# One encoder layer on one core: the first two feed-forward tiles in an order of their own, gate and up alternating

## The chip, the cores and the metric

One core of a Trainium2 chip runs the whole program. The time is that of one execution on the device in microseconds, from the first to the last instruction with what lies around them. The kernel before was run three times: 1383.03, 1385.15 and 1387.94 us, median 1385.15.

## The reference, cut to what matters

One layer is applied to 1088 tokens (1024 of a new stream, 64 of a running one), model width 1024, feed-forward width 2816, all in 32-bit floats:

```
xn   = rmsnorm(x, norm_mix)
proj = xn @ w_in                       # split into three kinds of token mixers
mix  = concat(hgrn2(...), s5(...), rglru(...))
x    = x + mix @ w_out                 # out projection
xn2  = rmsnorm(x, norm_ffn)
hid  = silu(xn2 @ w_gate) * (xn2 @ w_up)
x    = x + hid @ w_down
y    = rmsnorm(x, norm_final)
```

The change touches the first products of the input projection (the S5 branch's input u), the end of the out projection with the RMS factors of the second norm, and the first two of the 22 feed-forward tiles of 128 columns.

## The kernel before, in words

The tokens stand in the free dimension, in three groups: 0 and 1 of 384 tokens, 2 of 320. The model width is eight slices of 128 partitions. A 32-bit value is split into a rounded high part (written by a copy on ACT) and the low rest (a subtraction on DVE). A product of weights and activations is then three rounds of matmuls into one PSUM tile, called j = 0, 1, 2: high by high, high weight by low activation, low weight by high activation (`dense`, L128; `product`, L1363). TensorE's instructions run in the order in which they are written; a dependency from each to the one before fixes it (L67). The other engines' orders are made by the scheduler from the order in the text, an instruction's priority, and when it can run; `first()`, `soon()` and `tc.high_priority(offset)` move what stands inside them ahead by so many instructions (400 for WPRIO). A tile belongs to a tag with a number of buffers, and an instruction that writes a new tile waits until one of them is free.

**Start.** Group 2 is first. Its x comes in four transfers of two slices each; `xsplit` (L324) splits each slice into xh (ACT) and xl (DVE). `weights_part` (L110) fetches half a weight tile (four slices, 256 KB) into a buffer with tag raw (three of them), ACT makes the high part whi and a negated copy in wlo, and a DMA of POOL's queue adds the weights onto it. The loop at L1147 sets the order of loads and splits: the halves of the first u tile stand behind slices 1 and 5, both halves of the second at the end. `uproj` (L350) makes one product after the other, 24 matmuls each; for group 2 the rounds run over the first four slices and then the last four.

**Out projection and second norm.** `outproj` (L174) makes eight output slices; those of slices 0 and 1 are done together, then each slice's product, an addition on DVE, its square on ACT and its sum on DVE (`square_sum`, L205). For a group, `row_sums` (L216) adds over the partitions on PE, `inv_rms` (L232) makes one over the root in a chain of some fifteen small DVE instructions, `spread` (L248) puts it across the partitions with two matmuls. The chain of group 0 lies in `finish` (L983), beside the out projection of group 1; that of group 1 beside the out projection of group 2 (loop at about L1334: row sums and chain at step 1, spread at step 3).

**Feed-forward, first pair of tiles.** Two tiles of weights and groups 0 and 1 are multiplied as a 2 by 2 block matrix with seven products in place of eight (`quad`, L1390), on operands that are halves of the scaled activations, or their sums and differences: b11, b22, d1 = b21 - b11, s = b11 + b22, d2 = b12 - b22, r2 = b21 + b22, r1 = b11 + b12. `operand` (L1299) makes each in four slices: an addition into a buffer with tag xT (four of them, also used for t, u, the squares and x2prep), the high part on ACT, the low part on DVE. b11, d1, b22 and s are made beside the out projection of group 2 (`preps`, L1317), d2, r2 and r1 behind it (`preps_late`, L1325); the additions of r2 and r1 run on POOL, all others on DVE. `scaled` (L1292) multiplies the rows by the RMS factors first. In `quad` the four parts of a weight block are loaded once (`raws`, L1370: two in raw, two in rw), their five sums and differences are made on DVE (L1396), and `wsplit` (L1356) splits them; whi and wlo have five buffers. The order of products is b11, b22, s, d1, d2, r2, r1. t, the copy of the first sum, is made on ACT (L1407) and then changed by the second and third product; d1 is added onto the first sum's PSUM tile, so it comes behind the copy. For the first pair the quad of gate comes first, then the chain, spread and `x2prep` (L258) of group 2, then the quad of up, then four `plain` products (L1382) of group 2 with newly fetched weights. For all later pairs the group-2 products lie inside the quad.

Of the kernel before, what the change touches and what calls it, by code (L numbers as in the profile page):

```python
# [58 lines left out]
def trunk(ctx: ExitStack, tc: tile.TileContext, I: dict, O: list):  # L59
# [114 lines left out]
    def outproj(gi, pool, xpool, xbufs, psd):  # L174
# [8 lines left out]
        sacc = pool.tile([128, TMAX], F32, tag="sil" if gi == 2 else "sacc", name="sacc", bufs=2)  # L183
# [94 lines left out]
    with ExitStack() as ph1:  # L278
# [71 lines left out]
        def uproj(gi, parts):  # L350
            T = GROUPS[gi]["T"]
            hi, lo = xn[gi]
            for m in range(2):
                o = ps_mm()
                dense(o[:, :T], parts[m], lambda k: (hi[:, k, :T], lo[:, k, :T]),
                      key=(lambda s: (s[1] == 2, s[0] // 4, s[1])) if gi == 2 else None)
                with tc.high_priority(offset=WPRIO):
                    for s0, n, dst in u_cols(gi, m):
                        A.copy(dst, o[:, s0:s0 + n].rearrange("p (c t) -> p t c", t=8))
# [623 lines left out]
        def finish():  # L983
# [10 lines left out]
            diags = inv_rms(0, sc)  # L994
# [152 lines left out]
        for k in range(NK):  # L1147
# [3 lines left out]
            if k in (1, 5):  # L1151
                part(0, k - k % 4)
        part(1, 0)
        part(1, 4)
# [162 lines left out]
    def preps():  # L1317
# [5 lines left out]
        yield from operand("s", halves(bigtile("o_s")), b11, b22, OP.add)  # L1323

    def preps_late():  # L1325
        yield from operand("d2", halves(bigtile("o_d2")), b12, b22, OP.subtract)
# [6 lines left out]
    for i, _ in enumerate(outproj(2, p2, p2, 4, ps_d)):  # L1333
        if i == 1:  # L1334
            with first():
                diags = inv_rms(1, row_sums(1, [sums[1]], ps_t))
        if i == 3:
            spread(1, diags, ps_t, sums[1])
# [51 lines left out]
    def quad(src, m, post, with_g2):  # L1390
# [30 lines left out]
        if with_g2:  # L1421
            plain(w11 + single(a12), post, m)
            plain(single(a21) + w22, post, m + 1)
# [11 lines left out]
    for fi, nf in enumerate(ffg):  # L1435
# [18 lines left out]
        for m in range(f0, f0 + nf, 2):  # L1454
            sil = [p2.tile([128, NTOK], F32, tag="sil", name="sil", bufs=2) for _ in range(2)]
            quad(I["w_gate"], m, gated, m > 0)
            if m == 0:
                with first():
                    diags = inv_rms(2, row_sums(2, [sums[2]], ps_t))
                spread(2, diags, ps_t, sums[2])  # L1460
                weave(x2prep(2, p2, (bigtile("x2h2"), bigtile("x2l2"))))
            quad(I["w_up"], m, upped, m > 0)
            if m == 0:
                for src, post in ((I["w_gate"], gated), (I["w_up"], upped)):
                    for i in range(2):
                        plain(weights(src[i], False), post, i)
# [116 lines left out]
```

## Time and profile before, and how to read it

| | |
|---|---|
| median of three runs | 1385.15 us |
| the profiled execution | 1381.88 us |
| its span, first to last instruction | 1380.1 us |
| mean granted clock of TensorE | 0.95 of full speed |
| PE, DVE, ACT, POOL busy | 92%, 66%, 48%, 16% |

A line of a timeline has the start in us, the length in us, the engine, the line of the kernel, the operation, the tile written and those read, the shape and the number of instructions merged; in brackets is the idle time before it and what ended it. A line of groups has the count, the busy time in us and the mean of one in ns, then idle time. Matmuls overlap their neighbours, so the distance of starts, and not their length, is what one costs. PEclk is the granted clock as a share of 2.4 GHz.

### The profile page before, as it was taken

The page shows a single profiled execution, that of the slowest core. Times are in us where ns is not written, and L with a number is a line of the kernel's source. Part 1 is how long each engine was busy: PE and PEld are TensorE (multiplying, and loading weights), DVE is VectorE, ACT ScalarE, POOL GpSimd, SP SyncE. Part 2 cuts the span into 40 slices and gives each one's busy share as a digit, 9 for nine tenths or more (in the row PEclk, how much of TensorE's full clock was granted, in tenths as well). Part 3 has the DMA queues.
Part 4 walks back from the last instruction along what each step waited for, and adds up shares of the span by engine and source line. Part 5 has one row for each costly group of instructions (what it writes and reads, how often), then busy time and mean ns, then how long its engine had stood idle before and what let it go on. Part 6 is the DMA issues. An engine that isn't in the chain of part 4 may idle for free.

```text
span 1380.1 us, 21112 instructions
## 1 busy us (share of the span) xinstructions
PE 1275.0 (92%) x7608; PEld 1214.8 (88%) x7608; DVE 913.5 (66%) x2206; ACT 660.0 (48%) x1288; POOL 224.2 (16%) x278
## 2 busy tenths in 40 slices
PE   7987998989988999759999999999999999999995
PEld 7876897878777889659999999999999999999985
DVE  9875798857766668976475437543763476346687
ACT  7766657768885444434243224412442243133463
POOL 2334354424342000020100000010001000100000
PEclk8997999999998899779999999999999999999997
DMA  9977687768884346303812551254125412631543
GB/s 285 287 148 180 138 172 147 172 142 177 164 188 107 104 162 212 116 15 96 164 39 71 117 96 38 77 107 92 55 71 110 80 54 77 107 78 62 184 141 111
DMA packets 94330, 170.60 MB, mean 124 GB/s; under 512 B 11425, under 2 KB 31473, under 8 KB 94225
## 3 DMA queue, kind: packets, MB, share of 16 engines
q1 hardware_dynamic: 70080, 108.26, 25.9%
q0 software_dynamic: 24144, 60.99, 25.0%
q8 instruction: 60, 0.98, 0.3%
q14 instruction: 46, 0.37, 0.1%
HBM read 134.76 MB, written 33.86 MB: 122 GB/s over the span
## 4 chain that ended last, share of the span: by engine, by line
PE 51%; DVE 3%; DMA 1%; issue 1%; ACT 0%; DVEq 0%; ACTq 0%
PE q L76 51%; DMA res<-st 1%; DVE wlo L122 1%; DVE u L1429 0%; DVE dg L243 0%; DVE x1r L1353 0%; DVE hl L1452 0%; DVE u L1430 0%; DVE sil L1450 0%; ACT whi L1359 0%; DVE sacc L214 0%; DVE sc L150 0%; DVE sc L149 0%; DVE sc L148 0%; DVE x1r L1480 0%
## 5 line engine op out<-in xcount | busy, mean ns | idle before, releaser
L117 ACT CAST whi<-raw 128x512 fp32r<-128x512 f32 (+1 forms) x232 | 139.5, 607 | 101.0 <-PE q L76 40.9
L76 PE MATMUL mm<-xh,whi 128*128 128x384 f32 (+1 forms) x480 | 168.8, 360 | 17.9 <-ACT whi L117 9.9
L76 PE MATMUL q<-hl,whi 128*128 128x384 f32 (+1 forms) x528 | 173.2, 332 | 2.7 <-DVE hl L1452 2.7
L76 PE MATMUL q<-hh,whi 128*128 128x384 f32 (+1 forms) x528 | 172.9, 331 | 2.1 <-ACT hh L1451 1.7
L76 PE MATMUL mm<-xl,whi 128*128 128x384 f32 (+1 forms) x480 | 159.6, 340 | 4.5 <-DVE xl L332 4.5
L120 POOL DMA_DIRECT2D wlo<-in_w_in_dram x112 | 99.4, 971 | 211.9 <-ACT wlo L119 180.1
L1482 DVE COPY st<-q 128x384 f32<-128x384 f32 x80 | 41.4, 524 | 134.3 <-PE q L76 118.5
L1493 POOL DMA_DIRECT2D res<-st x40 | 34.0, 851 | 585.9 <-DVE st L1482 499.7
L76 PEld LDWEIGHTS mm<-xh,whi 128*128 128x128 f32 x480 | 95.3, 200 | 25.5 <-ACT whi L117 10.5
L76 PE MATMUL q<-hh,wlo 128*128 128x384 f32 (+1 forms) x528 | 111.7, 330 | 0.0
L1359 ACT CAST whi<-raw 128x512 fp32r<-128x512 f32 x128 | 78.1, 621 | 67.4 <-PE q L76 53.9
L1360 DVE TENSOR_TENSOR wlo<-raw,whi 128x512 fp32r<-128x512 f32 x128 | 87.5, 685 | 29.6 <-ACT whi L1359 14.2
L76 PEld LDWEIGHTS q<-hl,whi 128*128 128x128 f32 x528 | 100.3, 190 | 4.9 <-DVE hl L1452 4.9
L76 PE MATMUL q<-x2l,whi 128*128 128x320 f32 x352 | 103.8, 309 | 0.0
L76 PE MATMUL q<-x2h,whi 128*128 128x320 f32 x352 | 103.8, 309 | 0.0
L76 PEld LDWEIGHTS q<-hh,whi 128*128 128x128 f32 x528 | 100.1, 190 | 4.0 <-ACT hh L1451 3.6
L122 DVE TENSOR_TENSOR wlo<-raw,whi 128x512 fp32r<-128x512 f32 (+1 forms) x120 | 80.1, 672 | 34.3 <-ACT whi L117 29.4
L76 PEld LDWEIGHTS mm<-xl,whi 128*128 128x128 f32 x480 | 94.8, 198 | 9.0 <-DVE xl L332 6.0
L76 PE MATMUL mm<-xh,wlo 128*128 128x384 f32 (+1 forms) x480 | 93.4, 335 | 6.1 <-DMA wlo<-in_w_in_dram 6.0
L1396 DVE TENSOR_TENSOR sm<-raw 128x512 f32<-128x512 f32 x66 | 45.6, 691 | 75.0 <-DMA raw<-in_w_up_dram 57.3
L76 PEld LDWEIGHTS q<-hh,wlo 128*128 128x128 f32 x528 | 91.6, 190 | 0.0
L76 PEld LDWEIGHTS mm<-xh,wlo 128*128 128x128 f32 x480 | 82.5, 193 | 8.9 <-DMA wlo<-in_w_in_dram 8.7
(467 smaller groups left out, 2930.8 us busy)
## 6 DMA issues: line engine op xcount, KB each, us to landing
raw<-in_w_in_dram SPq DMA_DIRECT2D x112, 256.0 KB, 4.3
wlo<-in_w_in_dram POOLq DMA_DIRECT2D x112, 256.0 KB, 6.0
res<-st POOLq DMA_DIRECT2D x40, 544.0 KB, 6.0
raw<-in_w_down_dram SPq DMA_DIRECT2D x56, 256.0 KB, 2.7
raw<-in_w_out_dram SPq DMA_DIRECT2D x48, 256.0 KB, 3.1
raw<-in_w_gate_dram SPq DMA_DIRECT2D x48, 256.0 KB, 2.9
raw<-in_w_up_dram SPq DMA_DIRECT2D x48, 256.0 KB, 3.0
xg<-in_x_dram SPq DMA_DIRECT2D x8, 512.0 KB, 6.3
```

Of the source, the lines that this page charges most:

```text
L76: in_order(PE.matmul(out, lhsT, rhs, start=start, stop=stop, **kw).ins)
L117: ins = A.copy(hi[:, :n, :], raw[:, :n, :]).ins
L120: G.dma_start(lo[:, :n, :], src[:, h0:h0 + n, :], accum_op=OP.add)
L122: tt(lo[:, :n, :], raw[:, :n, :], hi[:, :n, :].bitcast(F32), op=OP.subtract)
L1359: A.copy(hi, src)
L1360: tt(lo, src, hi.bitcast(F32), op=OP.subtract)
L1396: tt(t_, a, b, op=op)
L1482: (A.copy if gi == 1 else V.tensor_copy)(st[:, t0:t0 + T], o[:, :T])
L1493: nc.gpsimd.dma_start(res[:, dm, :], st, accum_op=OP.add)
```

## The change

- The tile that holds the sum of squares of group 2 is taken from tag hh instead of sil.
- `uproj` for group 2 makes both products together: round 0 of the first four slices for both, of the last four for both, then round 1 for both, then round 2 for both. The load order alternates: first half of tile 0 behind slice 1, first half of tile 1 behind slice 3, second halves behind slices 5 and 7.
- The chain of group 0 in `finish` stands in `soon()`.
- The additions of s and d2 run on POOL.
- Row sums and chain of group 1 move to step 0 of the out projection of group 2, the spread to step 1, in `first()`.
- The first pair of tiles is made by a new function, `opening`, once for gate and once for up, in alternation, one product each per step. Its order is b11, d1, b22, s, d2, r2, r1. Each product fetches its own parts (alternately into rw and raw); the sums of weights are made on POOL. Row sums and chain of group 2 come before step 2, the spread before step 3, and x2prep behind all steps.

```diff
-        sacc = pool.tile([128, TMAX], F32, tag="sil" if gi == 2 else "sacc", name="sacc", bufs=2)
+        sacc = pool.tile([128, TMAX], F32, tag="hh" if gi == 2 else "sacc", name="sacc", bufs=4 if gi == 2 else 2)
...
+            os = [ps_mm() for _ in range(2)]
+            if gi == 2:
+                for ks, js in ((range(4), (0,)), (range(4, 8), (0,)), (range(8), (1,)), (range(8), (2,))):
+                    for m in range(2):
+                        for j in js:
+                            for k in ks:
+                                mm(os[m][:, :T], parts[m][k][j == 2], acts(k)[j == 1],
+                                   start=(j == 0 and k == 0), stop=(j == 2 and k == 7))
...
             sc = row_sums(0, [sums[0]], ps_mx)
-            diags = inv_rms(0, sc)
+            with soon():
+                diags = inv_rms(0, sc)
...
-            if k in (1, 5):
-                part(0, k - k % 4)
-        part(1, 0)
-        part(1, 4)
+            if k in (1, 3):
+                part(k // 2, 0)
+            if k in (5, 7):
+                part(k // 2 - 2, 4)
...
-        yield from operand("s", halves(bigtile("o_s")), b11, b22, OP.add)
+        yield from operand("s", halves(bigtile("o_s")), b11, b22, OP.add, G)
...
-        yield from operand("d2", halves(bigtile("o_d2")), b12, b22, OP.subtract)
+        yield from operand("d2", halves(bigtile("o_d2")), b12, b22, OP.subtract, G)
...
     for i, _ in enumerate(outproj(2, p2, p2, 4, ps_d)):
+        if i == 0:
+            with first():
+                diags = inv_rms(1, row_sums(1, [sums[1]], ps_t))
         if i == 1:
             with first():
-                diags = inv_rms(1, row_sums(1, [sums[1]], ps_t))
-        if i == 3:
-            spread(1, diags, ps_t, sums[1])
+                spread(1, diags, ps_t, sums[1])
...
+    def opening(src, post):
+        bufs = [0]
+        def fresh(dm, k):
+            bufs[0] += 1
+            pool, tag, n = ((wp, "raw", 3), (p2, "rw", 2))[bufs[0] % 2]
+            t_ = pool.tile([128, 4, 128], F32, tag=tag, name="raw", bufs=n)
+            nc.sync.dma_start(t_, src[dm][:, k:k + 4, :])
+            return t_
+        def summed(a, b, op):
+            with first():
+                x_, y_ = fresh(*a), fresh(*b)
+                G.tensor_tensor(x_, x_, y_, op=op)
+                return wsplit(x_)
+        a11, a12, a21, a22 = (0, 0), (0, 4), (1, 0), (1, 4)
+        oa, ob, oc = ps_q(), ps_q(), ps_q()
+        t_ = temp("t")
+        product(oa, summed(a21, a22, OP.add), "b11")
+        with first():
+            A.copy(t_, oa[:, :TMAX])
+        yield
+        product(oa, weights_part(src[1], 4)[0], "d1", False)
+        with first():
+            post(1, 0, oa[:, :TMAX])
+        yield
+        product(ob, summed(a11, a12, OP.add), "b22")
...
+        product(oc, summed(a11, a22, OP.add), "s")
...
+        product(ob, weights_part(src[0], 0)[0], "d2", False)
...
+        for x_, y_, name, acc, m, g in ((a12, a22, "r2", oa, 0, 0), (a21, a11, "r1", ob, 1, 1)):
+            o = ps_q()
+            product(o, summed(x_, y_, OP.subtract), name)
+            u = temp("u")
...
+            if m:
+                quad(I["w_gate"], m, gated)
+                quad(I["w_up"], m, upped)
+                continue
+            both = [opening(I["w_gate"], gated), opening(I["w_up"], upped)]
+            for i in range(7):
+                if i == 2:
+                    with first():
+                        diags = inv_rms(2, row_sums(2, [sums[2]], ps_t))
+                if i == 3:
+                    with first():
+                        spread(2, diags, ps_t, sums[2])
+                    run2 = x2prep(2, p2, (bigtile("x2h2"), bigtile("x2l2")))
+                for g in both:
+                    next(g)
+            for _ in run2:
+                pass
+            for src, post in ((I["w_gate"], gated), (I["w_up"], upped)):
+                for i in range(2):
+                    plain(weights(src[i], False), post, i)
```

## Rows read from the trace of the kernel before

**Rows 1.** The page, part 1: busy time, share of the span, instructions.
```profile
PE 1275.0 (92%) x7608; PEld 1214.8 (88%) x7608; DVE 913.5 (66%) x2206; ACT 660.0 (48%) x1288; POOL 224.2 (16%) x278
```

**Rows 2.** Busy time by stage: stretch, its length, each engine (instructions), PEclk, DMA share, GB/s.
```profile
0.00:24.60 24.60, 16.65 (x73) 14.47 (x74) 21.72 (x137) 14.90 (x30) 8.79 (x28) 0.72 0.91 265
...
500.00:535.70 35.70, 32.40 (x175) 31.00 (x173) 28.69 (x65) 16.86 (x35) 0.00 (x0) 0.95 0.58 189
...
566.70:600.30 33.60, 12.66 (x38) 9.06 (x36) 31.29 (x53) 15.14 (x31) 11.11 (x9) 0.61 0.15 52
600.30:634.40 34.10, 28.23 (x140) 27.46 (x141) 25.79 (x62) 13.54 (x26) 0.00 (x0) 0.88 0.19 55
634.40:681.00 46.60, 44.77 (x278) 43.84 (x276) 23.43 (x47) 15.10 (x33) 6.26 (x8) 1.00 0.66 128
```

**Rows 3.** PE's waits, 566 to 635 us: total us, times, longest us.
```profile
PE q L76 <- ACT t L1407: 14.2, 2, 12.1
PE q L76 <- issue: 5.0, 1, 5.0
PE q L76 <- DVE dg L243: 3.8, 1, 3.8
```

**Rows 4.** Timeline of ACT, 599 to 605 us.
```profile
599.38 0.51 ACT L1307 CAST o_r<-xs 128x384 fp32r<-128x384 f32 x1 [0.76 <-POOL xs L1305]
599.80 0.47 ACT L1407 COPY t<-q 128x384 f32<-128x384 f32 x1
```

**Rows 5.** Timeline of PE, 561 to 690 us.
```profile
568.15 0.86 PE L76 MATMUL q<-o_b,wlo 128*128 128x384 f32 x4
...
600.32 2.93 PE L76 MATMUL q<-o_d,whi 128*128 128x384 f32 x8 [12.14 <-ACT t L1407]
...
604.33 1.91 PE L76 MATMUL q<-o_d,whi 128*128 128x384 f32 x8
...
619.64 1.55 PE L76 MATMUL q<-o_b,whi 128*128 128x384 f32 x8
...
621.72 1.55 PE L76 MATMUL q<-o_s,whi 128*128 128x384 f32 x8
```

**Rows 6.** Timeline of PE, 0 to 55 us.
```profile
20.76 1.04 PE L76 MATMUL mm<-xh,whi 128*128 128x320 f32 x4
...
24.58 0.34 PE L76 MATMUL mm<-xh,whi 128*128 128x384 f32 x1
```

**Rows 7.** Timeline of PE, 500 to 690 us.
```profile
514.76 0.41 PE L76 MATMUL mx<-dg,ones_r 128*128 128x384 f32 x1 [1.39 <-DVE sc L241]
...
516.90 0.52 PE L76 MATMUL mm<-mh,whi 128*128 128x384 f32 x1
```

**Rows 8.** The same view, around row sums and spread of group 1.
```profile
542.84 0.72 PE L76 MATMUL q<-ones,sacc 128*128 128x1 f32 x6
...
551.72 0.44 PE L76 MATMUL q<-dg,ones_r 128*128 128x384 f32 x1 [1.01 <-DVE dg L243]
```

**Rows 9.** Groups of DVE instructions, 536 to 635 us, shapes kept apart.
```profile
L264 DVE SCALAR_TENSOR_TENSOR xT<-x,cols,sacc 128x320 f32<-128x320 f32 x8 | 4.1, 549 | 0.0
L1396 DVE TENSOR_TENSOR sm<-raw 128x512 f32<-128x512 f32 x6 | 4.1, 687 | 0.4 <-DMA raw<-in_w_up_dram 0.4
```

**Rows 10.** The tile o_r, 580 to 606 us: ns min/median/max, first and last start.
```profile
L1308 DVE TENSOR_TENSOR o_r<-xs,o_r x8: 545/1342/1346, 592.9 to 600.2; 128x384 fp32r<-128x384 f32 x8
```

**Rows 11.** Timeline of DVE, 540 to 690 us.
```profile
576.39 0.61 DVE L1295 SCALAR_TENSOR_TENSOR x<-x,cols,sacc 128x384 f32<-128x384 f32 x1
...
582.41 1.49 DVE L1308 TENSOR_TENSOR o_s<-xs,o_s 128x384 fp32r<-128x384 f32 x3
...
592.88 7.82 DVE L1308 TENSOR_TENSOR o_r<-xs,o_r 128x384 fp32r<-128x384 f32 x8
```

**Rows 12.** Timeline of POOL, 592 to 600 us.
```profile
593.04 6.31 POOL L1305 TENSOR_TENSOR xs<-x,x 128x384 f32<-128x384 f32 x5 [0.49 <-DVE o_d L1308]
```

**Rows 13.** DMA issues, 536 to 635 us: count, KB each, median us to landing.
```profile
raw<-in_w_gate_dram SPq DMA_DIRECT2D x10, 256.0 KB, 2.8
```

More of the change, by code (lines that the diff above doesn't have):

```diff
@@ L352, in uproj @@
             hi, lo = xn[gi]
+            acts = lambda k: (hi[:, k, :T], lo[:, k, :T])
+            os = [ps_mm() for _ in range(2)]
[6 more added lines that the diff above has]
+                                   start=(j == 0 and k == 0), stop=(j == 2 and k == 7))
             for m in range(2):
-                o = ps_mm()
-                dense(o[:, :T], parts[m], lambda k: (hi[:, k, :T], lo[:, k, :T]),
-                      key=(lambda s: (s[1] == 2, s[0] // 4, s[1])) if gi == 2 else None)
+                o = os[m]
+                if gi != 2:
+                    dense(o[:, :T], parts[m], acts)
                 with tc.high_priority(offset=WPRIO):
@@ L1388, in plain, with quad @@
             post(m, 2, o[:, :T])
-    def quad(src, m, post, with_g2):
+    def opening(src, post):
[24 more added lines that the diff above has]
+        with first():
+            tt(t_, ob[:, :TMAX], t_, op=OP.add)
+        yield
+        product(oc, summed(a11, a22, OP.add), "s")
+        with first():
+            tt(t_, oc[:, :TMAX], t_, op=OP.subtract)
+        yield
+        product(ob, weights_part(src[0], 0)[0], "d2", False)
+        with first():
+            post(0, 1, ob[:, :TMAX])
+        yield
+        for x_, y_, name, acc, m, g in ((a12, a22, "r2", oa, 0, 0), (a21, a11, "r1", ob, 1, 1)):
+            o = ps_q()
+            product(o, summed(x_, y_, OP.subtract), name)
+            u = temp("u")
+            with first():
+                tt(u, o[:, :TMAX], t_, op=OP.add)
+                tt(u, acc[:, :TMAX], u, op=OP.add)
+                post(m, g, u)
+            yield
+    def quad(src, m, post):
         a11, a12, a21, a22 = raws(src[m], src[m + 1])
@@ L1420, in quad @@
             post(m, 1, ob[:, :TMAX])
-        if with_g2:
-            plain(w11 + single(a12), post, m)
-            plain(single(a21) + w22, post, m + 1)
+        plain(w11 + single(a12), post, m)
+        plain(single(a21) + w22, post, m + 1)
         for x_, y_, name, acc, mm_, g in ((a12, a22, "r2", oa, m, 0), (a21, a11, "r1", ob, m + 1, 1)):
@@ L1455, in trunk @@
             sil = [p2.tile([128, NTOK], F32, tag="sil", name="sil", bufs=2) for _ in range(2)]
[L1456 to L1466, printed above, removed]
+            if m:
[5 more added lines that the diff above has]
+                if i == 2:
+                    with first():
+                        diags = inv_rms(2, row_sums(2, [sums[2]], ps_t))
+                if i == 3:
+                    with first():
+                        spread(2, diags, ps_t, sums[2])
[7 more added lines that the diff above has]
+                    plain(weights(src[i], False), post, i)
         last = fi == len(ffg) - 1
```

## The prediction

> **What bounds the kernel now.** I read the totals first, then the busy time by stage, then PE's waits in the weak stage, and last the single instructions around them. PE is busy 92% of the span [rows 1], so only its idle or slow stretches can give time. The stages show where they are [rows 2]. From 566.7 to 634.4 us, which is the opening pair of feed-forward tiles, PE is busy 12.66 of 33.60 us at clock 0.61 and then 28.23 of 34.10 at 0.88. The first 24.6 us have 16.65 busy, and 500 to 535.7 has 32.40 of 35.70. In the first half of the opening DVE is busy 31.29 of 33.60 us: the operands are what is late, not the weights' transfer. PE's longest wait there is 12.1 us for the copy t on ACT, then 5.0 and 3.8 us, the last for the RMS chain of group 2 [rows 3]. The reader should see in [rows 4] that the t copy started right behind the last of eight casts of the r operands, at 599.80, though the last four multiplications of the product that it reads began at 568.15 [rows 5]. The copy shares four buffers (tag xT) with the sums of all operands, so I read the delay as a queue for buffers.
>
> What a product costs: twelve multiplications from 619.64 to 621.72, 2.08 us at full clock; the first after the long wait took 600.32 to 604.33, 4.01 us at the lower clock of 1.2 GHz [rows 5]. The opening has 2 x 7 products, 29.1 us at full clock, and took 67.7. So 38 us are there, and the question is how many the operands let go.
>
> **The change part by part.**
>
> *First two products together.* The 24 multiplications of the second u product ran from 20.76 to 24.58, 3.8 us, after the first had waited for its inputs [rows 6]. Now 16 of them can fill the waits. All 3.8 us would be the gain if every wait were filled; but the low parts of the weights now arrive in another order: the second half of the first tile comes third instead of second, and its last group of multiplications needs it. A loss of 1 us bounds it on the other side. I take -1, near the small end, because the last input arrives when it did.
>
> *The RMS chain of group 0 put ahead (soon).* PE waits 1.4 us for its first half and again a little for the second, and some ten multiplications behind it stand 0.32 us apart instead of 0.17 (516.90 is the first of them listed, 0.52 us long against 0.33) [rows 7]: 1.4 + 0.5 + 1.5 = 3.4 us. Bounds 0 to -3.4; I take -3, since two dense products lie on PE between the sums and the spread, ample for a chain that another time made PE wait 3.8 us [rows 3] with no work between.
>
> *spread(1) moved from step 3 to step 1 of the out projection, row_sums to step 0.* PE's order is fixed by hand, and between the two there is now no PE work. In the trace they stand 8.9 us apart, with two dense products between [rows 8]. So PE stands still for the chain: at least 3.8 us, as its sister chain made it wait [rows 3], less what is ready early, call it 3; at most 8.2. I take +5. Behind it the whole queue of PE's out projection moves, weights and all. It is not in the sum below, where the operands, and not PE, set the end; the gain is that scaled(1), and all operands of the second group, may begin some 5 us earlier on DVE.
>
> *Sums on POOL.* Eight adds of s and d2, 128x384, leave DVE (the same shape: 545 ns alone [rows 10], three in 1.49 us, so 0.47 apart [rows 11]) for POOL, which made five such adds in 6.31 us, 1.26 each [rows 12]. Ten weight sums of 128x512 leave DVE (687 ns [rows 9]); none on POOL is in the trace. Bounds for one are 1.26 us, the smaller add, and 2.5, twice that; I take 1.7, four thirds, as the elements are. But the two engines do not run side by side: while POOL added, DVE's subtractions of the same shape took 1342 ns in the median instead of 545 and went at POOL's pace [rows 10 to 12]. So a pair of add and subtraction, 0.94 us on DVE alone, costs 1.26 between the two. For eight adds the 0.32 more make +2.6 us of shared time; for ten weight sums, four thirds of the 0.32 each, +4.3. I take +8 before the last operand is ready, one more because up's weight splits now come ahead of it too. Between the bounds of one sum it is 4 to 16. The Trainium skill (SBUF — State Buffer, "Who interferes with whom") says that a DVE instruction with two SBUF inputs and a GpSimd instruction that reads SBUF exclude one another, the second waiting out the first; the trace agrees (1.34 against 0.55 us). Without that rule, by the adds that leave DVE alone, the eight and ten would count as a gain of some 10 us.
>
> *Parts fetched per product.* 24 parts instead of 8 for the seven products of gate and up, 16 more of 256 KB, each landing in 2.8 us [rows 13] with the DMA engines busy 15% and 19% in the two halves [rows 2]. Nothing on the path as long as the five raw buffers rotate; what would be late if they do not is the POOL add, one product behind. On SP's queue they stand between the last out-projection weights and the plain products' parts, which are wanted 30 us later.
>
> *Gate and up alternating.* This is the main term. Each operand now feeds two products, so PE's work for b11, d1, b22, s and d2 lies beside the making of the next operands instead of half of it behind the last. x2prep, formerly between the quads, comes behind the opening: eight pairs of DVE instructions of half a microsecond each (549 ns the first of a pair [rows 9]), some 8 us. Part of it runs beside the last products; I charge 3.
>
> **The sum.** The last r operand was ready at 600.7 (592.88 + 7.82 [rows 11]). It moves by -4 (start and chain of group 0), +8 (POOL), -4 (spread(1) early, weight sums off DVE's own queue): 600.7 again. By then ten products can be issued; I leave six, since POOL also owes their weight sums: 6 x 2.08 = 12.5, 2 more at the lower clock, 3 for x2prep: 618.2 against 634.4, that is -16. The profiled execution took 1381.9 (span 1380.1), so 1366; the median of the runs shown is 3.3 us above it, so 1369. Behind the opening PE is busy 44.77 of 46.60 us at full clock [rows 2], so the gain is carried through.
>
> **The rivals.**
>
> *The t copies stay last* (0.27). As in the trace, they get a buffer only behind the sixteen operand sums; now both gate and up need one before the second pair. For: [rows 4], and the buffers are still four. Against: the sums are slower now, so that copies may come between. PE then holds 12 products at about 597: 25 + 2 for the clock + 2 for the chain of group 2 is 626, 8 us early: 1377.
>
> *DVE starved by POOL: slower* (0.16). From about 573 (scaled(1) ended at 577 [rows 11], less 4) DVE has 16 operand subtractions, 10 weight splits and 16 instructions of x2prep, all with two SBUF inputs. If POOL's 26 adds keep every one of them at 1.34 us [rows 10], that is 56 us, and 14 instructions on PSUM of 0.55 make it 637, plus the last pair 4.2: 641, 7 late: 1391. It decides from a mean of about 1.18 us for these 42. Against: POOL has 26 adds for 42 instructions. The Trainium skill speaks for it (GPSIMD Engine Reference, "4.1 Engine selection"): elementwise work on two inputs belongs on VectorE, GpSimd being about twice as slow; the trace agrees with 1.26 us to 545 ns, 2.3.
>
> *Nothing gained* (0.10): the shared time of DVE and POOL is the bound in both kernels, and what PE saves in the opening it waits for in x2prep; 1382 to 1386. The stage's DVE load [rows 2] speaks for it, the 5 us of chain wait and the late t copy against.
>
> *PE alone is the bound* (0.05): 14 x 2.08 from about 568 plus 2 us of small products ends near 599; with x2prep uncovered, 7 more: 606, 28 early, 1357.
>
> **How the numbers follow.** The forecast has 0.42 and its own range is 1362 to 1376: start and chains at their bounds, 7 us either way, about 1369. The range for 8 in 10 reaches over the t rival and part of "nothing", down to the PE-bound case: 1357 to 1388. A measurement of this kernel can tell about 0.3%, 4 us, from no change. Faster than 1381: forecast, t rival and PE-bound, less a little, 0.71; within: 0.13; slower: 0.16.
>
> **What would show it.** Right: between the out projection and the first plain product, o_b, o_d and o_s products come in pairs, the t copies stand before the r casts, and plain products start near 618. PE stands 3 to 8 us between row_sums(1) and spread(1) in the out projection. POOL's busy time in the stage rises from 11 to some 35 us and DVE's two-input instructions have means of 0.8 to 1.1 us. The wait of 1.4 us near 514 is gone. The prediction is wrong if PE's longest wait is still for t (first rival), if DVE's means pass 1.2 us (second rival), or if plain products wait for x2l by more than 5 us.

## The result and the profile after

The changed kernel is slower: 1400.26 us against 1386.55 (medians of four runs each, in turns on one chip), a ratio of 1.0096 with a 95% interval from 1.0074 to 1.0119. The two profiled executions are 18.0 us apart, 1399.91 and 1381.9.

The page of the changed kernel, part 1, then its busy time in the stretches of [rows 2], then PE's and POOL's waits (total, times, longest; PE from 570 to 645 us, POOL from 543 to 645):

```profile
PE 1277.3 (91%) x7608; PEld 1218.9 (87%) x7608; DVE 912.0 (65%) x2184; ACT 662.9 (47%) x1292; POOL 252.4 (18%) x300
```
```profile
0.00:24.60 24.60, 17.55 (x73) 14.29 (x74) 21.58 (x121) 14.84 (x30) 8.73 (x28) 0.86 0.91 258
...
566.70:600.30 33.60, 13.46 (x88) 13.14 (x86) 24.91 (x34) 15.35 (x31) 23.77 (x19) 0.76 0.59 170
600.30:634.40 34.10, 22.91 (x108) 22.36 (x109) 20.52 (x39) 12.04 (x22) 15.04 (x13) 0.74 0.35 92
634.40:681.00 46.60, 42.36 (x235) 40.12 (x234) 27.47 (x59) 17.04 (x37) 2.56 (x3) 0.89 0.42 102
```
```profile
PE q L76 <- issue: 29.3, 1, 29.3
PE q L76 <- ACT x2h L265: 2.7, 1, 2.7
PE q L76 <- DVE dg L243: 2.0, 2, 1.4
```
```profile
POOL res L1295 <- ACT sqt L211: 24.3, 1, 24.3
POOL raw L1414 <- DMA raw<-in_w_gate_dram: 14.4, 3, 5.9
POOL wlo L120 <- ACT wlo L119: 12.3, 4, 7.6
```

Against [rows 1] the reader sees the same work on PE and 28 us more on POOL, whose longest waits are for other engines and for transfers. Against [rows 2] the opening's second half has lost 5.3 us of PE time and the stretch behind it another 2.4, both at a lower clock. The waits of 12.1, 5.0 and 3.8 us [rows 3] have become one of 29.3 and two small ones. The long one is put down to "issue"; the timelines of PE, then ACT, tell what it is:

```profile
537.75 1.41 PE L76 MATMUL q<-mh,whi 128*128 128x320 f32 x8 [1.40 <-ACT o_b L1317]
...
551.96 1.35 PE L76 MATMUL q<-dg,ones_r 128*128 128x384 f32 x2 [6.37 <-DVE dg L243]
...
579.31 0.86 PE L76 MATMUL q<-o_b,wlo 128*128 128x384 f32 x4
609.46 2.90 PE L76 MATMUL q<-o_d,whi 128*128 128x384 f32 x8 [29.29 <-issue]
...
644.95 0.41 PE L76 MATMUL q<-x2h,whi 128*128 128x320 f32 x1 [2.70 <-ACT x2h L265]
...
665.79 0.34 PE L76 MATMUL q<-hh,whi 128*128 128x384 f32 x1
```
```profile
608.47 0.51 ACT L1317 CAST o_r<-xs 128x384 fp32r<-128x384 f32 x1 [0.76 <-POOL xs L1315]
608.89 0.85 ACT L1422 COPY t<-q 128x384 f32<-128x384 f32 x2
609.74 0.52 ACT L1317 CAST o_r<-xs 128x384 fp32r<-128x384 f32 x1
```

Both b11 products (tile o_b) are done by 580.2, and the copies of their sums into t (two in one line) still stand among the last casts of the r operands, as in [rows 4]. The next product, d1 (tile o_d), adds onto the same sums in PSUM, so it waits for the copy. Twelve of fourteen products are left for the time behind the operands.

From here on a stage is counted from 537.75, the first product of group 2 in the output projection, which has the same short wait for o_b in every profile, to the first hh product of the down projection. This stage took 128.04 us against 112.79 before (from 535.73 to 648.52), +15.25. The remaining 2.8 of the 18.0 lie ahead of it and behind it. Inside the stage, counted from its start: the last r operand is ready at 65.0 before and 73.1 after, +8.1; from there to the first plain product 33.7 and 34.1, +0.4; the 96 multiplications of the plain products 14.1 and 20.8, +6.8.

### The profile page after: what moved, and what is told of

Its sections match the earlier page's. It is cut to its first block, busy times and chain, and to the rows that moved or that the text cites. A ratio compares the mean times of both kernels' runs of the same rounds, so it can differ in the third digit from the quotient of the medians.

```text
span 1398.1 us, 21154 instructions
## 1 busy us (share of the span) xinstructions
PE 1277.3 (91%) x7608; PEld 1218.9 (87%) x7608; DVE 912.0 (65%) x2184; ACT 662.9 (47%) x1292; POOL 252.4 (18%) x300
## 4 chain that ended last, share of the span: by engine, by line
PE 64%; DVE 14%; issue 6%; DMA 6%; POOL 4%; ACT 3%; SPq 0%; DVEq 0%; ACTq 0%; POOLq 0%
PE q L76 51%; PE mm L76 8%; PE mx L76 5%; DVE wlo L122 1%; DMA raw<-in_w_out_dram 1%; DMA xraw<-in_xT_dram 1%; POOL wlo L120 1%; DMA wlo<-in_w_in_dram 1%; POOL xs L1315 1%; DMA res<-st 1%; DMA raw<-in_w_down_dram 1%; ACT whi L117 1%; DVE mix L1069 1%; ACT wlo L119 1%; ACT L138 1%
## 5 line engine op out<-in xcount | busy, mean ns | idle before, releaser
L76 PE MATMUL q<-o_d,whi 128*128 128x384 f32 x352 | 70.3, 342 | 30.9 <-issue 29.3
L76 PEld LDWEIGHTS q<-o_d,whi 128*128 128x128 f32 x352 | 63.5, 193 | 31.5 <-POOL xs L1315 29.6
```

Of the source, the lines that this page charges most:

```text
L76: in_order(PE.matmul(out, lhsT, rhs, start=start, stop=stop, **kw).ins)
```

## The experiments

All stages, counted in us from the stage's start, one profile each; the ratio is to the kernel before, beside which each was timed. Kernels of one paragraph were run together unless it says otherwise. The part of the span outside this stage differs between these profiles by up to 11 us (1263.7 in e8, 1275.0 in e16), so single steps are read from the stage and the whole from the ratio. The stage has a scatter of its own: e12, e15, e18 and e19 have the same code in it and took 107.2, 106.8, 104.3 and 106.2 us. A step of less than 3 us in one profile is therefore not told from scatter.

| kernel | last r operand | first plain product | stage | ratio, 95% interval |
|---|---|---|---|---|
| before | 65.0 | 98.7 | 112.8 | |
| after | 73.1 | 107.2 | 128.0 | 1.0096 [1.0074, 1.0119] |
| e1, t's own buffer | 80.6 | 100.7 | 120.9 | 1.0094 [1.0061, 1.0127] |
| e2, spread(1) back | 67.1 | 99.9 | 120.1 | 1.0077 [1.0052, 1.0103] |
| e3, old start | 73.7 | 106.4 | 126.5 | 1.0096 [1.0059, 1.0133] |
| e4, before with t's own buffer | 69.3 | 92.2 | 106.3 | 0.9948 [0.9926, 0.9970] |
| e5, weight sums on DVE | 69.8 | 101.4 | 122.9 | 1.0090 [1.0065, 1.0116] |
| e6, s and d2 on DVE | 69.1 | 103.1 | 123.9 | 1.0124 [1.0093, 1.0155] |
| e8, x2prep woven | 73.8 | 102.4 | 124.8 | 1.0103 [1.0075, 1.0132] |
| e9, no alternation | 71.3 | 116.0 | 130.1 | 1.0138 [1.0108, 1.0167] |
| e10, no adding DMAs | 71.1 | 106.1 | 127.0 | 1.0144 [1.0118, 1.0170] |
| e11, four edits | 74.0 | 85.7 | 108.4 | 1.0011 [0.9993, 1.0030] |
| e12, all edits | 79.1 | 82.2 | 107.2 | 0.9984 [0.9965, 1.0004] |
| e13, e12 with a later chain | 78.2 | 83.0 | 107.5 | 0.9988 [0.9969, 1.0006] |
| e14, before with the new start | 64.7 | 99.4 | 113.4 | 1.0014 [0.9995, 1.0033] |
| e15, e12 with the old start | 78.4 | 81.6 | 106.8 | 0.9928 [0.9901, 0.9955] |
| e16, e12 without alternation | 69.2 | 94.7 | 108.8 | 0.9999 [0.9981, 1.0018] |
| e17, e16 with one pair, old start | 67.7 | 92.8 | 110.3 | 0.9996 [0.9975, 1.0016] |
| e18, e15 with the hurried chain | 76.8 | 79.9 | 104.3 | 0.9940 [0.9917, 0.9964] |
| e19, e15 with the products together | 78.2 | 82.6 | 106.2 | 0.9981 [0.9960, 1.0003] |

### Who holds the products: t's buffer, spread(1), the start (e1 to e4)

e1, and the same in e4 on the kernel before:
```diff
-        t_ = temp("t")
+        t_ = p2.tile([128, TMAX], F32, tag="hl", name="t", bufs=4)
```


> The changed kernel with t of the opening in buffers of its own (two of the four of tag hl that stand free there) instead of the four of tag xT. Theory Q: PE's wait of 29.3 us before the d1 products is the t copies' queue for an xT buffer behind the sixteen operand sums. Then the copies follow the b11 products near 580, PE does the d1, b22 and s products between the operands, and only what needs the last operand (ready near 610) is left: the last r product ends near 615 to 622 instead of 642, the time falls by 15 to 25 us against the changed kernel, to 1376 to 1385. Theory P: the time that POOL and DVE share sets the end whatever t does; the wait moves to the operands, the last r product still ends at 638 or later and the time stays within 5 us of 1400.

> The kernel before with t of the first pair's two quads in buffers of its own (tag hl). Theory Q: the wait of 12.1 us for t before the d1 product and that of 2.0 us in the quad of up go; the products d1 and d2 of gate then wait for the d2 operand only, so 5 to 12 us are gained: 1374 to 1381. Theory P: PE's wait moves to the d2 and r operands, and since those are ready at 593 and 601, the time stays within 3 us of 1386.

The PE timeline of e1, then pieces of its DVE timeline, then from e4 the end of gate's first product on PE and its t copy on ACT:
```profile
585.66 2.52 PE L76 MATMUL q<-o_d,whi 128*128 128x384 f32 x8 [4.29 <-issue]
...
591.50 0.71 PE L76 MATMUL q<-ones,sacc 128*128 128x1 f32 x6
...
615.33 0.64 PE L76 MATMUL q<-dg,ones_r 128*128 128x320 f32 x1 [18.69 <-DVE dg L243]
```
```profile
598.70 0.14 DVE L226 COPY sc<-q 128x2 f32<-128x2 f32 x1
...
602.45 3.61 DVE L148 TENSOR_TENSOR sc<-sc 128x3 f32<-128x3 f32 x1
...
608.08 0.54 DVE L1318 TENSOR_TENSOR o_r<-xs,o_r 128x384 fp32r<-128x384 f32 x1
...
613.93 1.35 DVE L243 TENSOR_TENSOR dg<-ident,sh 128x384 fp32r<-128x384 f32 x1
```
```profile
576.53 0.86 PE L76 MATMUL q<-o_b,wlo 128*128 128x384 f32 x4
577.43 0.48 ACT L1407 COPY t<-q 128x384 f32<-128x384 f32 x1
```
The wait of 29.3 us is gone, so it was the queue for buffers. The same edit puts the copy of the kernel before directly behind its product, takes the 12.1 us out and makes that kernel faster (e4, 7.2 us by the ratio, within the 5 to 12 of theory Q). In the changed kernel a wait of 18.7 takes the place of the 29.3: the chain of group 2 now starts while the operands are made, its links stand between them in DVE's order (one of three elements takes 3.61 us there, 0.16 in the kernel before), and the last operand comes 7.5 us later. The stage is 7.2 us shorter, but neither theory's range was met: the last r product ends at 635.8, and the ratio is the changed kernel's. So e4, and not e1, shows by its time that the wait costs.

e2 puts row_sums(1) and spread(1) back into steps 1 and 3 of the output projection. e3 undoes the first two products together (each again a whole dense product) and their loads:
```diff
-        if i == 0:
+        if i == 1:
             with first():
                 diags = inv_rms(1, row_sums(1, [sums[1]], ps_t))
-        if i == 1:
-            with first():
-                spread(1, diags, ps_t, sums[1])
+        if i == 3:
+            spread(1, diags, ps_t, sums[1])
...
-            if k in (1, 3):
-                part(k // 2, 0)
-            if k in (5, 7):
-                part(k // 2 - 2, 4)
+            if k in (1, 5):
+                part(0, k - k % 4)
+        part(1, 0)
+        part(1, 4)
```


> The changed kernel with row sums and chain of group 1 at step 1 and its spread at step 3 of the out projection, as before the change. Both theories: PE's wait of 6.4 us between row sums and spread goes (and the slower clock behind it), so the out projection ends some 7 us earlier. Theory Q: what POOL does sets the end of the opening, and the operands of group 1's rows come later, so of these 7 us nearly nothing reaches the end: within 3 us of 1400. Rival R: PE's standing in the out projection is passed on in full: 1393.

> The changed kernel with the start of before: one u product after the other and the old order of loads. The row sums of group 0 came at 508.1 instead of 504.2 us. If the new start causes this shift of 3.9 us, they come near 504 again, and since everything behind follows PE and DVE, the time falls by 2 to 4 us, to 1396 to 1398. If the shift is scatter of the stages between, the time stays at 1400 within 1.5 us.

e2 gains 7.9 us of stage, more than the stall of 6.37 and what rival R expected of the time; the ratio falls by 0.0019 only, less than the intervals can tell. PE's granted clock behind the stall, 0.53 from 552 to 557 us, adds to the stall. POOL's order shows how an early stall of PE can reach the operands; first the changed kernel, then e2:
```profile
582.76 0.80 POOL L1295 DMA_DIRECT2D res<-x  x1
583.57 1.01 POOL L1315 TENSOR_TENSOR xs<-x,x 128x384 f32<-128x384 f32 x1
587.19 1.26 POOL L1414 TENSOR_TENSOR raw<-raw 128x512 f32<-128x512 f32 x1 [2.61 <-DMA raw<-in_w_gate_dram]
...
603.38 1.57 POOL L1414 TENSOR_TENSOR raw<-raw 128x512 f32<-128x512 f32 x1
604.91 4.79 POOL L1315 TENSOR_TENSOR xs<-x,x 128x384 f32<-128x384 f32 x4
```
```profile
578.18 0.80 POOL L1295 DMA_DIRECT2D res<-x  x1 [2.71 <-DVE x L189]
581.11 2.48 POOL L1413 TENSOR_TENSOR raw<-raw 128x512 f32<-128x512 f32 x2 [2.13 <-DMA raw<-in_w_gate_dram]
583.56 4.92 POOL L1315 TENSOR_TENSOR xs<-x,x 128x384 f32<-128x384 f32 x4
```
The adds of s, now POOL's, stand behind the write of group 2's residual rows (res), which needs the output projection's last results. In e2 these results and the write come 5.8 us earlier in the stage. The first add comes only 1.2 us earlier, since POOL makes two weight sums first; but the last one ends 6.0 us earlier, since from the first to the last POOL then needs 21.3 us for 16 adds and one weight sum, where the changed kernel needs 26.1 for 16 adds, three weight sums and a wait of 2.61 for a weight transfer. That the write is what passes the stall on is read from this order; no run took it out of POOL's queue. The old start (e3) changes the stage by 1.5 us, within the scatter, and the ratio not at all.

### Who makes the operands late, and what alternation gives (e5, e6, e8, e9)

The diffs of e5 (weight sums on DVE), e6 (adds of s and d2 on DVE), e8 (x2prep advances in the openings' last steps) and e9 (gate's opening whole, then chain, spread and x2prep, then up's):
```diff
-                G.tensor_tensor(x_, x_, y_, op=op)
+                tt(x_, x_, y_, op=op)
...
-    ... operand("s", halves(bigtile("o_s")), b11, b22, OP.add, G)
+    ... operand("s", halves(bigtile("o_s")), b11, b22, OP.add)
-    ... operand("d2", halves(bigtile("o_d2")), b12, b22, OP.subtract, G)
+    ... operand("d2", halves(bigtile("o_d2")), b12, b22, OP.subtract)
...
                 for g in both:
                     next(g)
+                    if i > 3:
+                        next(run2, None)
...
+            for _ in both[0]:
+                pass
             for i in range(7):
...
-                    run2 = x2prep(2, p2, (bigtile("x2h2"), bigtile("x2l2")))
-                for g in both:
-                    next(g)
-            for _ in run2:
-                pass
+                    weave(x2prep(2, p2, (bigtile("x2h2"), bigtile("x2l2"))))
+                next(both[1])
```


> The changed kernel with the 12 weight sums of the openings on DVE in place of POOL; nothing else. In the changed kernel POOL's order holds the operand s's first add until 583.6, behind weight sums that wait for their transfers, and spends some 19 us on the sums. Theory P (POOL's queue with its sums, and the time that it shares with DVE, sets when the last operand is there): POOL's adds of s begin with x at about 573 to 577, the t copies behind them at 600 to 604 in place of 608.9, ratio 1.003 to 1.007. Theory Q (the t copies wait for an xT buffer, so for the end of the operands, whoever adds): the copies still stand right behind the last operand casts; the time follows them. Rival D (DVE is what paces the operands: 12 sums of about 0.7 us more on it): the copies at 609 to 617, ratio 1.010 to 1.016.

> The changed kernel with the adds of the operands s and d2 back on DVE (8 adds), as in the kernel before; r1, r2 and the weight sums stay on POOL. Theory P: the s operand no longer waits for POOL's queue (583.6 in the changed kernel), the last operand 2 to 6 us earlier, ratio 1.004 to 1.008. Rival D (DVE paces): 8 adds of 0.5 to 0.6 us more on DVE, the last operand up to 4 us later, ratio 1.010 to 1.013. The wait of some 29 us ahead of the first d1 product stays a single one under both, since its t copy still waits for an xT buffer.

> The changed kernel with the second norm's scaling of group 2 (24 operations, x2prep) put between the last three steps of the openings, in place of behind them all. In the changed kernel the plain products begin 2.7 us after the last product, run with small waits at a reduced clock (23.7 us for what took 14.1 before). Theory X (the scaling exposed behind the openings costs 8 to 10 us): the wait of 2.7 and the small ones go, the first product of x2h with wlo comes 6 to 9 us earlier counted from row_sums(1), ratio 1.003 to 1.005. Rival (the plain products wait for their weights, or the clock is what is lost): less than 3 us, ratio 1.007 to 1.010.

> The changed kernel without the alternation: the whole opening of gate, then the chain, spread and scaling of group 2, then the whole opening of up; fetches, POOL sums and order inside an opening stay. Theory of the forecast (alternation gives products to run while the operands are still made): the wait ahead of the operands' end longer by four products' time, 10 to 12 us, offset by the scaling of group 2 hidden again behind up's products (8 to 10 us): ratio 1.009 to 1.014. Theory Q (with t in the xT queue alternation gives nothing: only the two b11 products run ahead): one product fewer ahead, 3 us, and the scaling hidden: ratio 1.002 to 1.006.

The openings have ten weight sums, not twelve as e5's text says. Taking them (e5) or the adds of s and d2 (e6) off POOL brings the last operand 3.3 and 4.0 us earlier and the stage 5.2 and 4.1 us shorter, in the direction of theory P. The times do not confirm it: e5's ratio lies between the ranges of P and D, and e6's, which should have fallen, in that of rival D. So what POOL's sums cost rests on one profile each. Weaving x2prep shortens the stage by 3.3 us; counted from row_sums(1), as its expectation does, the first product of x2h with wlo comes 2.8 us earlier, where 6 to 9 were expected and under 3 was the rival's sign. The first plain product comes 4.8 us earlier, but the plain products then take 22.3 us instead of 20.8. Without alternation the stage is 2.1 us longer, within the scatter, and the ratio lies in the range of the forecast's theory: the first plain product comes 8.8 us later, and the plain products are back at 14.1 us, with x2prep hidden as before. The time of the plain products, with PE's clock as the column behind POOL, in the changed kernel and then in e12:
```profile
644.95:655.00 10.05, 8.51 (x25) 6.58 (x26) 7.62 (x17) 4.57 (x10) 0.00 (x0) 0.52 0.05 18
655.00:665.79 10.79, 10.79 (x73) 10.79 (x72) 3.79 (x8) 3.99 (x9) 0.00 (x0) 0.97 0.27 74
```
```profile
620.80:632.75 11.95, 6.82 (x17) 3.78 (x17) 11.36 (x26) 5.61 (x12) 0.00 (x0) 0.69 0.13 45
632.75:645.81 13.06, 13.06 (x82) 13.06 (x81) 4.49 (x9) 4.61 (x10) 0.00 (x0) 0.89 0.21 62
```
The first of the four plain products pays: it takes its inputs as x2prep makes them, and PE is granted the lower clock meanwhile.

### The edits together (e10 to e13)

e10 makes the low halves of the opening's d1 and d2 parts on DVE in place of an adding DMA that POOL issues. e11 is e1, e2, e8 and e10 together; e12 adds e5 and e6, so that of the change there remain the own order, the alternation, the fetches and the start; e13 moves the chain of group 2 one step later.
```diff
-        product(oa, weights_part(src[1], 4)[0], "d1", False)
+        product(oa, weights_part(src[1], 4, add=False)[0], "d1", False)
...
-        product(ob, weights_part(src[0], 0)[0], "d2", False)
+        product(ob, weights_part(src[0], 0, add=False)[0], "d2", False)
...
-                if i == 2:
+                if i == 3:
                     with first():
                         diags = inv_rms(2, row_sums(2, [sums[2]], ps_t))
-                if i == 3:
+                if i == 4:
```

> The changed kernel with the low halves of the opening's d1 and d2 parts made by a subtraction on DVE (4 of 0.7 us) in place of ACT's negation and an adding DMA that POOL issues. In the changed kernel POOL stands before two of these DMAs for 3.81 us at 576.4 and issues them for 0.9 us each, ahead of operand s. Theory P (POOL's queue sets the start of s and with it the end of the operands): s begins 4 to 6 us earlier, the t copies at 603 to 606 in place of 608.9, the stage from the out projection's first mh product behind operand o_b (537.75) to the first hh product (665.79), 128.0 us in the changed kernel, takes 122 to 125; ratio 1.005 to 1.008. Rival (weight sums and their transfers hold the queue anyway): stage 127 to 128, ratio 1.008 to 1.011.

> Four edits together on the changed kernel: the opening's t out of the xT buffers (7.2 us of the stage alone), row_sums(1) and spread(1) back in their old steps (7.9), the scaling of group 2 between the last steps (3.3), the d1 and d2 parts without adding DMAs. If the three known savings were separate losses: stage 128.0 - 18.4 = 109.6, under the 112.8 of the kernel before, ratio 0.996 to 0.999. If they are the same idle time of PE seen three times (operands end at the same time whichever wait is removed): stage 117 to 121, ratio 1.002 to 1.007.

> The kernel with the four edits, and besides the adds of s and d2 and the weight sums on DVE: of the change there remain the own order, the alternation, the fetches per product and the start. Theory of the forecast (alternation is worth 16 us if operands come in time): stage 98 to 104, ratio 0.990 to 0.994. Theory P (DVE and POOL together have the same work and set the end; alternation only moves the idle time): stage 108 to 114, ratio 0.997 to 1.002. Rival D (DVE as the pace, 20 adds more on it than in the kernel with the four edits): stage longer than that kernel's by 3 to 8.

> As the kernel with all edits, with the chain and spread of group 2 one step later (steps 3 and 4 of the openings in place of 2 and 3). With t out of the xT buffers PE stood 18.7 us before spread(2), whose chain ran between the operands' DVE work. Theory C (the chain's place in DVE's order costs): the wait for spread(2) under 4 us, stage 3 to 8 us shorter than with the chain in step 2, unless the scaling behind it is exposed by as much. Theory P: the same within 2 us, since PE then waits for the operands instead.

Without the adding DMAs the stage is 1.0 us shorter, as the rival said and within the scatter; POOL's order waits for other things too. The ratio, 1.0144, lies above both ranges. In the stage the other three savings add up as separate losses: 128.0 - 7.2 - 7.9 - 3.3 - 1.0 = 108.6, measured 108.4, closer than the scatter lets one expect. The time follows, from 1.0096 to 1.0011, but misses the 0.996 to 0.999 of separate losses, though the stage is 4.4 us shorter than before. e12's stage just misses theory P's range on the short side and its ratio lies in it; the forecast's theory and rival D fail. e12 shows what the forecast had in mind, in its PE timeline:
```profile
587.25 1.31 PE L76 MATMUL q<-ones,sacc 128*128 128x1 f32 x6 [8.39 <-DVE sacc L214]
...
596.55 0.42 PE L76 MATMUL q<-dg,ones_r 128*128 128x320 f32 x1 [2.34 <-DVE dg L243]
...
613.27 0.44 PE L76 MATMUL q<-o_r,whi 128*128 128x384 f32 x1 [1.90 <-DVE o_r L1318]
...
620.12 0.85 PE L76 MATMUL q<-o_r,wlo 128*128 128x384 f32 x4
620.81 0.31 PE L76 MATMUL q<-x2h,whi 128*128 128x320 f32 x1
```
Only 7.5 us of products are left behind the last wait for an operand, and the first plain product comes 16.5 us earlier in the stage than before. But the last operand is 14.1 us later and the plain products take 25.0 us instead of 14.1. The step later (e13) changes nothing, as theory P said.

### What remained open: the start and the alternation (e14 to e19)

e14 is the kernel before with the first two products together, their loads in turns and the hurried chain of group 0; e15 is e12 with all of these undone; e16 is e12 with e9's order; e17 is e16 with the old start and up's first product put between row_sums(2) and spread(2). e18 and e19, run together later, put the hurried chain or the products and loads back into e15. The hurried chain, then e17's own line:
```diff
-            diags = inv_rms(0, sc)
+            with soon():
+                diags = inv_rms(0, sc)
...
                     with first():
                         diags = inv_rms(2, row_sums(2, [sums[2]], ps_t))
+                    next(both[1])
                     with first():
                         spread(2, diags, ps_t, sums[2])
```


> The kernel before with the start of the change alone: the first two products of group 2 together, weight parts loaded in turns, the chain of group 0 hurried. The forecast's terms: -1 and -3 us, ratio 0.997. Theory S (the start costs 2 to 4 us, which the profiles' scatter of some 7 us at this place hides): ratio 1.0015 to 1.003. Theory N (nothing either way): 0.999 to 1.001.

> The kernel with all edits, and the old start besides: the products one after the other, the old loads, the chain of group 0 not hurried. Theory S: the 5.6 us that the opening's stage is shorter than in the kernel before come through, ratio 0.995 to 0.997. Theory N: as the kernel with all edits, 0.998 to 0.9995, and what eats the stage's gain stays open. Forecast's terms: 1.001 to 1.002.

> The kernel with all edits without the alternation: gate's opening whole, then chain, spread and scaling of group 2, then up's. Stage with all edits 107.2, kernel before 112.8. The forecast's main term (alternation is worth some 16 us in time): stage 116 to 124, ratio 1.005 to 1.011. Theory P (DVE's and POOL's work sets the end of the operands, alternation moves PE's idle time and exposes the scaling by as much): stage 105 to 110, ratio 0.997 to 1.000.

> As the kernel without alternation and with the old start, but up's first product stands between row_sums(2) and spread(2), so that it covers the chain of group 2 (3.8 us of waiting in the kernel before, 6.6 in the changed kernel without alternation). Theory P: the wait for spread(2) falls under 2 us, stage 103 to 107, ratio 0.993 to 0.997. Rival (the alternation of all products is worth more than this one): stage longer than 108, ratio above 0.998.

> The kernel with all edits and the old start (0.9928), with the chain of group 0 hurried again, the old products and loads kept. If the hurried chain costs: 0.996 to 0.999, and the waits at spread(0) no shorter than 1.0 and 0.5 us. If the products and their loads cost: 0.991 to 0.995. The forecast's term for the hurried chain, -3 us: 0.990 to 0.991.

> The kernel with all edits and the old start, with the first two products of group 2 together and the loads in turns again, the chain of group 0 not hurried. If the products and their loads cost: 0.996 to 0.999, row_sums(0) some 3 us later than with the old start (504 to 506 us in three of four profiles with the old start, 507 to 510 with the new). If the chain costs: 0.991 to 0.995. The forecast's term, -1 us: 0.992.

e18 is faster than e19 by 1372.66 against 1376.78 us; the ratios are 0.0041 apart, plus or minus 0.0032 by their intervals. So by the times the products together and their loads cost, and the hurried chain does not (0.9928 without it, 0.9940 with it). PE's waits from 60 to 200 us, first e18, then e19:
```profile
PE mm L76 <- ACT whi L117: 8.1, 1, 8.1
PE mm L76 <- DMA wlo<-in_w_in_dram: 5.7, 4, 2.6
PE mx L76 <- DVE sMV L883: 3.3, 1, 3.3
PE mm L76 <- DVE hlast L535: 1.0, 1, 1.0
```
```profile
PE mm L76 <- ACT whi L117: 9.4, 1, 9.4
PE mx L76 <- DVE xc L496: 3.7, 1, 3.7
PE mx L76 <- DVE sMV L892: 3.6, 1, 3.6
PE mm L76 <- DMA wlo<-in_w_in_dram: 2.9, 2, 2.1
PE mm L76 <- DVE xr L415: 1.5, 1, 1.5
PE mm L76 <- DVE g L457: 1.2, 1, 1.2
```
Up to 60 us the waits fall from 10.5 to 8.1, as they were meant to (in the changed kernel PE is busy 17.55 of the first 24.6 us, 16.65 before [rows 2]); here they rise from 18.1 to 22.3, by new waits for DVE's convolution and gating (xc, xr, g). row_sums(0) then starts at 505.06 in e18 and 507.24 in e19. All twenty profiles agree on these waits: from 60 to 200 us PE waits 16.0 to 20.3 us in the six with the old products and loads and 21.3 to 23.2 in the fourteen with the new.

How the waits become time is not shown. The stage starts at 536.40 in e18 and 536.17 in e19, so the lead of 2.2 us at row_sums(0) is gone by then, and of the 2.1 us between the two profiles' spans 2.0 lie in the stage, whose code is the same. Nor is the place of row_sums(0) the sign that e19's text takes it for: it stands at 505.5 in e8 and 513.6 in e16 with the new start, at 511.9 in e4 with the old. What speaks for a cost besides e18 and e19 is a sum over the table. The ratio less one, times the median of the kernel before, is the change in time; less the change of the stage, 1.3 to 6.0 us are left over in the thirteen experiments with the new products and loads, and -4.0 to 2.0 in the five with the old. The changed kernel itself, with -1.9, does not fit. An estimate from these means is some 4 us, but the size stays open: e14's interval includes no change, and e3 showed none.

Alternation, once t is free, is worth 1.6 us of stage (e12 against e16), which is within the scatter; the ratios' intervals overlap too. Its parts are larger: it brings the first plain product 12.5 us earlier, makes the last operand 9.9 us later, and lengthens the plain products by 10.9. From the stage's start to the last operand DVE makes 37 weight splits and sums in e12 and 31 in e16, and the chain of group 2 besides. That is theory P. e17 missed: the wait for spread(2) is still 3.52 us, and stage (110.3) and ratio came as its rival said, though that rival's reason, a worth of full alternation, is not borne out by e12 against e16. e15 and e18 are the fastest kernels here, e15 faster than any of its expectations; e4, one line on the kernel before, follows with 0.9948 and needs none of the rest. The intervals of the three overlap.

## Why the prediction was wrong

**Forecast and rivals.** The direction was wrong and 1400.3 lies above the range. The mechanism was that of the first rival, which had 0.27: the t copies stay last. Its price failed. "PE then holds 12 products at about 597: 25 + 2 for the clock + 2" would have ended at 626; they began at 609.46, and the first plain product at 644.95. So a rival put on the fast side names the longest wait of the slower kernel.

**The step that failed first is in the sum: "-4 (start and chain of group 0)" and "-4 (spread(1) early, weight sums off DVE's own queue)".** Neither came. They were to cancel the +8 for sums on POOL, so that the last operand stood at its old place; it came 8.1 us later in the stage, and the stage itself began 2.0 us later. That 8.1 is near the +8 is luck: e2, with all sums still on POOL, leaves only 2.1 of it, so most came from spread(1), which was to gain, while e5 and e6 take off 3.3 and 4.0. How much the sums alone cost was not separated. The start gave nothing and by e18 and e19 rather costs; the hurried chain left PE's wait at spread(0) at 1.10 us where it had been 1.39 [rows 7].

**spread(1).** The stall was foreseen at +5 (3 to 8.2) and measured 6.37, but left "not in the sum" because operands and not PE set the end. e2 shows it in full in the stage, and 6.0 us of it at the last operand. What the step missed is, as far as POOL's order shows it, a queue: s and d2 moved to POOL stand behind the residual write and among the weight sums, so they wait for the output projection, and PE's stall there is a stall of the operands.

**The larger miss: "By then ten products can be issued; I leave six."** Two were issued and twelve left. From the last operand to the first plain product the sum had 17.5 us (12.5 + 2 + 3); it took 34.1, against 33.7 before, so the main term of 16 us did not come at all. The argument against the rival, that slower sums let the copies in between, failed: the copies came among the last casts. I had read the queue for buffers rightly in [rows 4] and then let the change escape it, though it takes two t's from the same four buffers. e1 shows that one tag removes the wait; it also shows that the next thing late is the chain of group 2, for which the forecast's sum had no term.

**x2prep at 3 us.** This term was too small. The plain products took 6.8 us longer, behind a wait of 2.7: 9.5. The scaling starts behind the last u (the addition behind the last r product), as DVE's order shows in the changed kernel:
```profile
643.39 0.55 DVE L1446 TENSOR_TENSOR u<-q,u 128x384 f32<-128x384 f32 x1
643.86 0.54 DVE L264 SCALAR_TENSOR_TENSOR xT<-x,cols,sacc 128x320 f32<-128x320 f32 x1
```

**The second rival** (DVE starved by POOL, 1391) was on the right side with another mechanism: DVE's subtractions of the operands had means of 1.00 to 1.10 us, under its point of 1.18, and DVE was less busy than before (24.91 of 33.60 us against 31.29). POOL's own order was the pace, as the casts that wait 0.76 us for POOL show above. "Nothing gained" was nearest to the truth about alternation itself: in e12 and e16 DVE is busy 31.13 and 30.28 of 34.10 us in the second half, and moving PE's work changes the stage by 1.6 us.

**What held:** the products in pairs, POOL's busy time in the stage (38.8 us, about 35 expected), and 1.26 us for POOL's add. PE never waited for the parts fetched per product, but POOL did, 14.4 and 3.2 us in four waits, and 2.61 of it lies among the adds of s, ahead of the last operand.

## What to carry to other kernels

A stall that "does not matter because another engine sets the end" must be followed through every queue that the change moves work into: here POOL's adds had been put behind a write that needs the stalled engine's results. Before products are reordered to fill a wait, look which buffer the first one's result needs; one tag was worth more here than the whole reordering. And work that fills PE earlier also asks DVE for its inputs earlier: count what it pushes behind it.

## What was not expected of the hardware

POOL's sum of 128x512 was expected at 1.7 us and took 1.25 to 1.61 in the changed kernel, once 3.24 (the first of two at 577.04); its add of 128x384 took 0.99 to 1.44 us, and in the longest run, from 598.32, the starts are 1.27 apart. Beside those runs DVE's subtraction had means of 1.00 to 1.10 us, and the last one, when POOL had finished, took 0.56. POOL is thus not of one speed either; what sets it was not separated here.
